# Split weights at drawn offsets in a two-pair ring, operands in unevenly placed groups, in a one-core transformer layer

## The chip, the core and the metric

The kernel runs on one core of a Trainium2 chip. The core has a matrix engine (TensorE, here PE, with its weight loads shown apart as PEld), a vector engine (VectorE, DVE), a scalar engine (ScalarE, ACT), GpSimd (POOL) and a sync engine (SP) that issues the DMAs here. Each works through its own queue in order, and semaphores order the queues against each other. The metric is the device time of one execution in microseconds.

## The reference

One layer of an encoder with 512 tokens and width 2048, all in float32. A conditioning vector gives six modulation vectors. A normalised input is projected to two groups of heads, eight HGRN2 heads (a gated linear recurrence) and eight stick-breaking attention heads. Their outputs go through an output projection and a gated residual. A SwiGLU feed-forward of width 5632 follows.

```python
def reference(x, c, norm1_g, w_in, hg_lb_logits, hg_out_g, sb_q_g, sb_k_g, sb_out_g,
              w_out, norm2_g, w_ffn_in, w_ffn_out, w_ada, b_ada):
...
    for layer in range(DEPTH):
        mod = cond @ w_ada[layer] + b_ada[layer]
        sh1, sc1, g1, sh2, sc2, g2 = [m[:, None, :] for m in jnp.split(mod, N_MOD, axis=-1)]

        h = rms_norm(x, norm1_g[layer]) * (1.0 + sc1) + sh1
        proj = h @ w_in[layer]
        hg_q, hg_f, hg_i, hg_g, sb_q, sb_k, sb_v = jnp.split(proj, IN_SPLITS, axis=-1)
        o_hg = hgrn2_mixer(hg_q, hg_f, hg_i, hg_g, lower_bounds[layer], hg_out_g[layer])
        o_sb = stick_breaking_mixer(sb_q, sb_k, sb_v, sb_q_g[layer], sb_k_g[layer], sb_out_g[layer])
        mixed = jnp.concatenate([o_hg, o_sb], axis=-1).astype(x.dtype) @ w_out[layer]
        x = x + g1 * mixed

        h = rms_norm(x, norm2_g[layer]) * (1.0 + sc2) + sh2
        gate, up = jnp.split(h @ w_ffn_in[layer], 2, axis=-1)
        x = x + g2 * ((jax.nn.silu(gate) * up) @ w_ffn_out[layer])
    return x
```

## The kernel before

Every large product is made from float32 values that are split in two: a high part, which a cast on ACT rounds to the matrix engine's float32r, and a low part, value minus high, which DVE subtracts. Three matmuls stand for one: high weight by high activation, high weight by low activation, low weight by high activation. The method `matmul` of class `Timed` (line 93) issues them all, so all of PE's float32r matmuls have line 93 in the profile, and only the tiles tell them apart.

**Weights.** A raw weight tile of up to 8 KB a partition comes by DMA from SP into one of four buffers (`raw_tile`, line 171, pool `wp`). `split` (line 212) takes one pair of tiles, tags `hi` and `lo`, casts on ACT (line 220) and subtracts on DVE (line 221). The pool has three buffers of each tag (line 137), so three split pairs exist at a time, and a fourth cast must wait until PE has left a slot. A slot is any free one, so a pair may be held. A split holds at most 1024 values a partition. In the feed-forward stages every fourth split goes to a further pair instead: `spare_here` (line 1105, tags `hi2` and `lo2` of pool `tp`) in the first one, `spare_there` (line 1165) in the second, there inside the operand tile `opsB`. The splits stand under a priority raised by `AHEAD` = 300 instructions, and a planner at build time puts the instructions of each engine in an order by priority and by when they are ready in its own model of time. On the chip each queue then keeps that order.

**Stages in order.** (1) v projection of HGRN, 16 steps, 512 columns, accumulators `st`. (2) attention projections, `sb_project` (line 337), 8 heads of 8 splits with 24 matmuls of 384 columns each. (3) HGRN projections, `mtile` (line 599), 8 heads of three products, two splits each with 24 matmuls of 512 columns. The attention and HGRN heads run beside this, set among the matmuls by a clock that the program itself keeps (`Clock`, line 102). (4) output projection, `wo_part` (line 808): for output tiles 0 and 1 all rows but those of the last HGRN head are done first, and their split weights are kept; the upper halves of tiles 2 and 3 follow; when the last head is finished, the kept pairs are used for its row and the loop at line 857 goes on. The activations of stages 1 to 4 lie in two tiles, `hhi` and `hlo` (later `ohi` and `olo`), of 16 rows of 512 values. (5) the gate and up products of the first two blocks of 128 columns (`first_part`, line 959), where the weights of chunk c serve first the first half of the tokens and, after the first product of chunk c + 1, the second half. (6) the first feed-forward stage: for 42 further blocks f, seven products by Strassen's scheme over halves of 8 row tiles (`product`, line 908), each with its own split of 1024 values and 24 matmuls of 256 columns. Their activation operands lie in `opA` (products 1 and 2), `opD` (3), `opB` (6 and 7) and `opC` (5 and 4), high and low alternating by row tile. Results leave PSUM by `tap` (ACT, line 1018), and the forms of the product go out to memory by DMA (line 1095). (7) the second feed-forward stage, `multiply` (line 1183): 12 units, four with three and eight with four tiles of 128 rows, again seven products each, with splits of up to two tiles; a two-tile split is used by 12 matmuls of 512 columns. Here the split weights are the moving operand, and the feed-forward operands, loaded back into `opsA`, `opsB` and `opsC` (`load_op`, line 1028), are the stationary one.

**Where the tiles lie.** This is the compiled program's allocation, in bytes from the start of a partition; the remainder by 512 stands in brackets. Ring, high parts: 43808, 47904, 52000. Ring, low parts: 56096, 60192, 64288 (288 each). `hhi`, `ohi`, `opB`, `opsC`: 68384 (288). `hlo`, `olo`, `opC`, `opsB`: 101152 (288). `opA`, `opsA`: 133920 (288). `opD`: 166688 (288). Spare pair of stage 6: 215008 and 219104 (480). Rows and blocks within them are whole multiples of 512 bytes, so the remainder is the same all through a tile.

Of the kernel before, what the change touches and what calls it, by code (L numbers as in the profile page):

```python
# [10 lines left out]
F32 = mybir.dt.float32  # L11
F32R = mybir.dt.float32r
# [5 lines left out]
P = 128  # L18
D = 2048
KT = 16  # L20
T = 512
# [3 lines left out]
HT = 256  # L25
HALF = 8
# [59 lines left out]
class Timed:  # L86


    def __init__(self, engine, clock):
        self.engine, self.clock = engine, clock  # L90
# [39 lines left out]
def trunk(ctx, tc, a):  # L130
    nc = tc.nc
    V, S, G = nc.vector, nc.scalar, nc.gpsimd
# [74 lines left out]
        nc.sync.dma_start(r, src)  # L207
        return r

    spare, count = [], [0]  # L210

    def split(r, shape, name):
        count[0] += 1
        if spare and count[0] % 4 == 0:
            hi, lo = spare[0](shape, name)
        else:
            hi = wp.tile(shape, F32R, tag="hi", name=name + "h")
            lo = wp.tile(shape, F32R, tag="lo", name=name + "l")
        with tc.high_priority(offset=AHEAD):
            S.copy(hi, r)  # L220
            V.tensor_sub(lo, r, hi.bitcast(F32))  # L221
        return hi, lo
# [30 lines left out]
        newton(y, av, tmp)  # L253


    hhi = hp.tile([P, KT, T], F32R, tag="hhi", name="hhi")
    hlo = hp.tile([P, KT, T], F32R, tag="hlo", name="hlo")
    xo = xop.tile([P, KT, T], F32, tag="xo", name="xo")
    vctx = ctx.enter_context(ExitStack())
    vp = vctx.enter_context(tc.tile_pool(name="vp", bufs=1))  # L260
# [25 lines left out]
    for k in range(KT):  # L286
        xk = xo[:, k]
        if k == 0:
            for i in range(2):
                sl = slice(i * 1024, i * 1024 + 1024)  # L290
                gemv(r0[:, sl], cond[:, sl], lead[:, i:i + 1])
            j = SC1 * KT
            V.scalar_tensor_tensor(mod[:, j:j + 1], lead[:, 0:1], lead[:, 1:2], small_col(C_BADA, j), op0=ALU.add, op1=ALU.add)
            finish_gain(SC1, 0, 1)
            whi = wp.tile([P, 1024], F32R, tag="hi", name="wi0h")
            wlo = wp.tile([P, 1024], F32R, tag="lo", name="wi0l")
# [12 lines left out]
        S.activation(hhi[:, k], xk, AF.Identity, scale=gk)  # L309
        V.scalar_tensor_tensor(hlo[:, k], xk, gk, hhi[:, k].bitcast(F32), op0=ALU.mult, op1=ALU.subtract)  # L310
        if k == 0:
            S.activation(ss1, xk, AF.Square)
        else:
            sq = sb.tile([P, T], F32, tag="qT" if k % 2 else "kT", name=f"sq{k}", bufs=1)
            S.activation(sq, xk, AF.Square)
            V.tensor_add(ss1, ss1, sq)
        for n in range(2):
            for t in range(4):
                ts_ = slice(t * P, t * P + P)
                cs = slice(n * T, n * T + T)  # L320
# [471 lines left out]
        gates[h] = SG  # L792


    ohi = hp.tile([P, KT, T], F32R, tag="hhi", name="ohi")
    olo = hp.tile([P, KT, T], F32R, tag="hlo", name="olo")
    last = NH - 1

    def split_o(k):
# [73 lines left out]

    early = fh.tile([P, 2, HALF, 2, HT], F32R, tag="b1", name="opA")
    H = {1: early[:, 0], 2: early[:, 1], 3: fg.tile([P, HALF, 2, HT], F32R, tag="b22", name="opD")}
    parts = {}

    def block(kh, th, j):  # L880
        return x1[:, kh * HALF + j, th * HT:th * HT + HT]

    def split_to(p, j, src):
        S.copy(H[p][:, j, 0], src)
        V.tensor_sub(H[p][:, j, 1], src, H[p][:, j, 0].bitcast(F32))

    def normed(kh, th, j):
        k, hs = kh * HALF + j, slice(th * HT, th * HT + HT)
# [3 lines left out]
    def make_first(j):  # L892
        for kh in range(2):
            normed(kh, 0, j)
            split_to(1 + kh, j, block(kh, 0, j))
            parts[kh, 0, j] = H[1 + kh][:, j, 0], H[1 + kh][:, j, 1]

    def make_second(j):
        normed(0, 1, j)
        t = ft.tile([P, 2, HT], F32R, tag="t", name=f"b12_{j}")  # L900
        S.copy(t[:, 0], block(0, 1, j))
        V.tensor_sub(t[:, 1], block(0, 1, j), t[:, 0].bitcast(F32))
        parts[0, 1, j] = t[:, 0], t[:, 1]
        normed(1, 1, j)
        split_to(3, j, block(1, 1, j))
        parts[1, 1, j] = H[3][:, j, 0], H[3][:, j, 1]

    def product(out, w, p, first=False):
        whi, wlo = w
        for j in range(HALF):  # L910
            PE.matmul(out, whi[:, j], H[p][:, j, 0], start=first and j == 0, stop=False, skip_group_check=True)
            PE.matmul(out, whi[:, j], H[p][:, j, 1], start=False, stop=False, skip_group_check=True)
            PE.matmul(out, wlo[:, j], H[p][:, j, 0], start=False, stop=j == HALF - 1, skip_group_check=True)

# [66 lines left out]
            with tc.high_priority(offset=AHEAD):  # L981
                hold(0)

    late = hp.tile([P, 2, HALF, 2, HT], F32R, tag="hhi", name="opB")
    later = hp.tile([P, 2, HALF, 2, HT], F32R, tag="hlo", name="opC")
    H.update({6: late[:, 0], 7: late[:, 1], 5: later[:, 0], 4: later[:, 1]})
    for j in range(HALF):
        V.tensor_sub(block(0, 0, j), block(0, 1, j), block(0, 0, j))
        t2 = ft.tile([P, HT], F32, tag="t", name=f"t2_{j}")
# [33 lines left out]

    def place(n):
        n %= 11
        return places[0][:, n] if n < 4 else places[1][:, n - 4] if n < 7 else places[2][:, n - 7]

    def load_op(c, q):
        if c < len(CHUNKS):
# [12 lines left out]
    yraw = []  # L1042

    def begin_second():
        places.append(fh.tile([P, 4, 4, 2, HT], F32R, tag="b1", name="opsA"))
        load_op(0, 0)
        load_y(0, 2)
        load_op(0, 1)
        load_y(0, 0)
        yraw.append(hp.tile([P, 3, 4, T], F32, tag="hhi", name="yraw0"))  # L1050
        load_y(0, 1)
        load_y(0, 3)
        load_op(0, 2)
        load_op(0, 3)
        places.append(hp.tile([P, 4, 4, 2, HT], F32R, tag="hlo", name="opsB"))
        for q in range(4, 7):
            load_op(0, q)
        yraw.append(fg.tile([P, 2, 4, T], F32, tag="b22", name="yraw"))
# [44 lines left out]
            later.pop(0)()  # L1103

    def spare_here(shape, name):
        return [tp.tile(shape, F32R, tag=t, name=name + t, bufs=1) for t in ("hi2", "lo2")]

    spare.append(spare_here)
    count[0] = 0
# [50 lines left out]
    tctx.close()  # L1160


    more = places[1][:, 3].rearrange("p n h t -> p (n h t)")

    def spare_there(shape, name):
        n = shape[1] * shape[2]
# [63 lines left out]
    for u, (c, i) in enumerate(units):  # L1230
# [15 lines left out]
        for q, p in enumerate(ORDER):  # L1246
# [37 lines left out]
            if p == 3:  # L1284
                load_y(u + 1, 3)
            if u == 0 and q == 6:
                places.append(hp.tile([P, 4, 4, 2, HT], F32R, tag="hhi", name="opsC"))
            if q < 4 and i == (c == 0):
                load_op(c + 1, q)
            if i == 1 and 1 <= q < 4:  # L1290
# [61 lines left out]
```

## Time and profile before

| | us |
|---|---|
| runs | 2303.31 and 2305.09 |
| median of the runs | 2304.2 |
| span of the profiled execution | 2299.2 |

The profiled execution's span runs from its first to its last instruction; its own time with what lies around the span is not listed apart, so the span is set against the median of the runs, which is 5.0 us more. The mean granted clock of PE over the span is 0.994 of full speed.

How to read the rows: in the timeline, a row gives the start in microseconds from the beginning of the span, the length, the engine, the line, the operation, the written tile and the read ones, the shapes, and how many like instructions the row merges; in brackets stands how long the engine was idle just before and what released it. Matmuls are pipelined, so their lengths overlap; what counts is from start to start. A name like `ff_5h` is product 5's high weights in the first feed-forward stage; `wfo_2h` those of the second stage for the tiles from 2 on.

### The profile page before, as it was taken

What the parts mean: (1) busy time and instruction counts of PE and PEld (TensorE: products, weight loads), DVE (VectorE), ACT (ScalarE), POOL (GpSimd) and SP (SyncE); (2) the same over time, 40 slices, a digit from 0 to 9 for tenths busy, and PEclk for the clock granted to TensorE, in tenths of its full rate; (3) what the DMA queues carried; (4) which work ended last, traced back from release to release, by engine and by line L of the source; (5) the groups of instructions that cost most, each with busy time, mean ns of one, the idle gap of its engine ahead of it and who ended that gap; (6) DMA issues with size and microseconds to landing.
All of it is one profiled execution on the core that took longest, in us unless ns stands there. A gap on an engine that the chain in (4) does not pass through costs nothing.

```text
span 2299.2 us, 35729 instructions
## 1 busy us (share of the span) xinstructions
PE 2249.4 (98%) x14171; PEld 2050.2 (89%) x14171; DVE 1917.8 (83%) x2566; ACT 1160.6 (50%) x2015; POOL 10.7 (0%) x25
## 2 busy tenths in 40 slices
PE   7999899999999999999999999999999999999999
PEld 6899899888888788999999999999999977778787
DVE  8887779999888865699899988888888778888888
ACT  4316666565655522564454445454545544544453
POOL 0000000000000000000000000000000000000000
PEclk9999999999999999999999999999999999999999
DMA  9885546853322386346555645454443486665452
GB/s 368 319 317 218 174 145 227 304 183 111 128 93 74 130 303 214 105 151 225 189 204 185 220 143 175 143 174 143 150 160 129 166 314 232 238 220 213 154 200 76
DMA packets 114978, 437.69 MB, mean 190 GB/s; under 512 B 9822, under 2 KB 58236, under 8 KB 76796
## 3 DMA queue, kind: packets, MB, share of 16 engines
q1 hardware_dynamic: 114812, 435.42, 53.0%
q8 instruction: 111, 1.82, 0.3%
q14 instruction: 55, 0.45, 0.1%
HBM read 386.61 MB, written 48.77 MB: 189 GB/s over the span
## 4 chain that ended last, share of the span: by engine, by line
PE 77%; DVE 13%; DMA 3%; issue 3%; ACT 3%; SPq 0%; DVEq 0%; ACTq 0%
PE ffA L93 18%; PE foA L93 9%; PE ffC L93 9%; PE sbp L93 7%; PE wo L93 7%; PE foC L93 4%; PE ffB L93 4%; PE st L93 4%; PE hgf L93 4%; PE hgq L93 3%; PE hgg L93 3%; DMA opd<-fhi 1%; DVE ada L180 1%; DVE yraw L1190 1%; PE l L93 1%
## 5 line engine op out<-in xcount | busy, mean ns | idle before, releaser
L180 DVE SCALAR_TENSOR_TENSOR ada<-ada,cond 128x2048 f32<-128x2048 f32 x95 | 216.8, 2286 | 54.5 <-DMA ada<-in_w_ada 54.3
L93 PE MATMUL ffA<-opD,ff_3h 128*128 128x256 f32 x512 | 93.9, 284 | 1.8 <-ACT u L1018 1.7
L93 PE MATMUL ffA<-opB,ff_6h 128*128 128x256 f32 x512 | 94.1, 284 | 1.0 <-ACT ff_6h L220 1.0
L93 PE MATMUL ffB<-opA,ff_2h 128*128 128x256 f32 x512 | 93.5, 283 | 0.0
L93 PE MATMUL ffC<-opC,ff_4h 128*128 128x256 f32 x512 | 93.5, 283 | 0.0
L93 PE MATMUL ffA<-opC,ff_5h 128*128 128x256 f32 x496 | 90.7, 283 | 0.8 <-ACT b L1018 0.8
L93 PE MATMUL ffA<-opA,ff_1h 128*128 128x256 f32 x496 | 90.6, 283 | 0.0
L93 PE MATMUL ffC<-opB,ff_7h 128*128 128x256 f32 x496 | 90.6, 283 | 0.0
L221 DVE TENSOR_TENSOR wfo_0l<-wfo,wfo_0h 128x1024 fp32r<-128x1024 f32 x48 | 58.7, 1224 | 37.9 <-ACT wfo_0h L220 37.5
L93 PEld LDWEIGHTS ffA<-opD,ff_3h 128*128 128x128 f32 x512 | 79.7, 192 | 2.4 <-ACT u L1018 2.4
L93 PEld LDWEIGHTS ffA<-opB,ff_6h 128*128 128x128 f32 x512 | 80.1, 193 | 1.3 <-ACT ff_6h L220 1.2
L93 PEld LDWEIGHTS ffC<-opC,ff_4h 128*128 128x128 f32 x512 | 79.7, 192 | 0.0
L93 PEld LDWEIGHTS ffB<-opA,ff_2h 128*128 128x128 f32 x512 | 79.7, 192 | 0.0
L220 ACT CAST wfo_0h<-wfo 128x1024 fp32r<-128x1024 f32 x48 | 50.6, 1054 | 57.5 <-PE foA L93 50.4
L1092 ACT CAST fhi<-forms 128x512 fp32r<-128x512 f32 (+1 forms) x63 | 43.6, 692 | 68.5 <-DMA opd<-fhi 59.2
L93 PEld LDWEIGHTS ffA<-opC,ff_5h 128*128 128x128 f32 x496 | 77.2, 192 | 1.0 <-ACT b L1018 1.0
L93 PEld LDWEIGHTS ffC<-opB,ff_7h 128*128 128x128 f32 x496 | 77.3, 192 | 0.0
L93 PEld LDWEIGHTS ffA<-opA,ff_1h 128*128 128x128 f32 x496 | 77.2, 192 | 0.0
L93 PE MATMUL ffA<-opB,ff_6l 128*128 128x256 f32 x256 | 72.7, 284 | 0.0
L93 PE MATMUL ffC<-opC,ff_4l 128*128 128x256 f32 x256 | 72.4, 283 | 0.0
L93 PE MATMUL ffA<-opD,ff_3l 128*128 128x256 f32 x256 | 72.4, 283 | 0.0
L93 PE MATMUL ffB<-opA,ff_2l 128*128 128x256 f32 x256 | 72.4, 283 | 0.0
(1646 smaller groups left out, 7764.6 us busy)
## 6 DMA issues: line engine op xcount, KB each, us to landing
ada<-in_w_ada SPq DMA_DIRECT2D x95, 1024.0 KB, 5.2
wfo<-in_w_fo SPq DMA_DIRECT2D x16, 1024.0 KB, 5.9
yraw<-in_w_fo SPq DMA_DIRECT2D x16, 1024.0 KB, 4.8
fix<-in_w_fix SPq DMA_DIRECT2D x14, 1024.0 KB, 5.6
opd<-forms SPq DMA_DIRECT2D x44, 256.0 KB, 4.3
opd<-fhi SPq DMA_DIRECT2D x42, 256.0 KB, 4.3
opsC<-opd SPq DMA_DIRECT2D x10, 1024.0 KB, 5.1
opsA<-opd SPq DMA_DIRECT2D x9, 1024.0 KB, 7.2
```

The source lines that it names most:

```text
L93: self.engine.matmul(out, lhsT, rhs, **kw)
L180: V.scalar_tensor_tensor(w, w, 1.0, row, op0=ALU.mult, op1=ALU.mult, accum_out=col)
L220: S.copy(hi, r)
L221: V.tensor_sub(lo, r, hi.bitcast(F32))
L1092: S.copy(hi, R[:, q])
L1190: V.tensor_sub(*(t[:, k0:k0 + w] for t in (d, e, g)))
```

## The change

The ring in `wp` has two buffers of each tag instead of three (the pool's own number is overridden in `pair_of`). Each is wider, 1144 values instead of 1024, and a split lies in it at an offset drawn at build time from 0 to 15 lines of 8 values (32 bytes); in about half of the draws the low part has the offset of the high part. The spare pair of stage 6 is drawn likewise. The tiles of activations and of feed-forward operands get 128 values more and are cut into two or four groups, each set off by a number of lines of its own, as the tuples in the diff say. High and low operands of products 3 to 7 become separate blocks, where they alternated before. What is computed, and the number of casts, subtractions, matmuls and DMAs, stays as it was.

```diff
-    spare, count = [], [0]
+    spare, count, draw = [], [0], np.random.RandomState(7)
+    LINE = 8
+    SLOT = 1024 + 15 * LINE
+
+    def shifted(t, off, shape):
+        n = int(np.prod(shape[1:]))
+        t = t[:, off:off + n]
...
+        return t
+
+    def pair_of(pool, tags, shape, name, bufs):
+        offs = draw.randint(0, 16, 2)
+        if draw.randint(0, 2):
+            offs[1] = offs[0]
+        return [shifted(pool.tile([P, SLOT], F32R, tag=tag, name=name + tag, bufs=bufs), LINE * int(o), shape)
+                for tag, o in zip(tags, offs)]
+
+    BIG = KT * T + 128
+
+    def grouped(tag, name, n, offs, shape, pool=None, size=BIG):
+        t = (pool or hp).tile([P, size], F32R, tag=tag, name=name)
+        return [shifted(t, i * n + LINE * o, [P] + shape) for i, o in enumerate(offs)]
+
+    class Rows:
...
+            v = self.views[k // 4][:, k % 4]
...
+    def rows_of(tag, name, offs):
+        return Rows(grouped(tag, name, 4 * T, offs, [4, T]))
...
     def split(r, shape, name):
         count[0] += 1
         if spare and count[0] % 4 == 0:
             hi, lo = spare[0](shape, name)
         else:
-            hi = wp.tile(shape, F32R, tag="hi", name=name + "h")
-            lo = wp.tile(shape, F32R, tag="lo", name=name + "l")
+            hi, lo = pair_of(wp, ("hi", "lo"), shape, name, 2)
...
-    hhi = hp.tile([P, KT, T], F32R, tag="hhi", name="hhi")
-    hlo = hp.tile([P, KT, T], F32R, tag="hlo", name="hlo")
+    hhi = rows_of("hhi", "hhi", (0, 1, 3, 6))
+    hlo = rows_of("hlo", "hlo", (0, 1, 3, 8))
...
-    ohi = hp.tile([P, KT, T], F32R, tag="hhi", name="ohi")
-    olo = hp.tile([P, KT, T], F32R, tag="hlo", name="olo")
+    ohi = rows_of("hhi", "ohi", (0, 2, 5, 12))
+    olo = rows_of("hlo", "olo", (0, 2, 5, 10))
...
-    early = fh.tile([P, 2, HALF, 2, HT], F32R, tag="b1", name="opA")
-    H = {1: early[:, 0], 2: early[:, 1], 3: fg.tile([P, HALF, 2, HT], F32R, tag="b22", name="opD")}
+    H = dict(zip((1, 2), grouped("b1", "opA", 4096, (0, 3), [HALF, 2, HT], fh)))
+    H[3] = grouped("b22", "opD", 2048, (5, 7), [HALF, HT], fg, 4096 + 128)
+    for p in (1, 2):
+        H[p] = [H[p][:, :, i] for i in range(2)]
...
-            PE.matmul(out, whi[:, j], H[p][:, j, 0], start=first and j == 0, stop=False, skip_group_check=True)
+            PE.matmul(out, whi[:, j], H[p][0][:, j], start=first and j == 0, stop=False, skip_group_check=True)
...
-    late = hp.tile([P, 2, HALF, 2, HT], F32R, tag="hhi", name="opB")
-    later = hp.tile([P, 2, HALF, 2, HT], F32R, tag="hlo", name="opC")
-    H.update({6: late[:, 0], 7: late[:, 1], 5: later[:, 0], 4: later[:, 1]})
+    late = grouped("hhi", "opB", 2048, (1, 1, 9, 9), [HALF, HT])
+    later = grouped("hlo", "opC", 2048, (2, 2, 4, 12), [HALF, HT])
+    H.update({6: late[0:2], 7: late[2:4], 5: later[0:2], 4: later[2:4]})
...
-        places.append(fh.tile([P, 4, 4, 2, HT], F32R, tag="b1", name="opsA"))
+        places.append(grouped("b1", "opsA", 2048, (0, 3, 6, 10), [4, 2, HT], fh))
...
-        places.append(hp.tile([P, 4, 4, 2, HT], F32R, tag="hlo", name="opsB"))
+        places.append(grouped("hlo", "opsB", 2048, (0, 2, 5, 9), [4, 2, HT]))
...
     def spare_here(shape, name):
-        return [tp.tile(shape, F32R, tag=t, name=name + t, bufs=1) for t in ("hi2", "lo2")]
+        return pair_of(tp, ("hi2", "lo2"), shape, name, 1)
...
-    more = places[1][:, 3].rearrange("p n h t -> p (n h t)")
+    more = places[1][3].rearrange("p n h t -> p (n h t)")
...
-                places.append(hp.tile([P, 4, 4, 2, HT], F32R, tag="hhi", name="opsC"))
+                places.append(grouped("hhi", "opsC", 2048, (0, 1, 4, 12), [4, 2, HT]))
```

More of the change, by code (lines that the diff above doesn't have):

```diff
@@ L208, in load, with __init__, __getitem__ @@
         return r
-    spare, count = [], [0]
+    spare, count, draw = [], [0], np.random.RandomState(7)
[4 more added lines that the diff above has]
+        t = t[:, off:off + n]
+        if len(shape) == 3:
+            t = t.rearrange("p (a b) -> p a b", a=shape[1])
+        elif len(shape) == 4:
+            t = t.rearrange("p (a b c) -> p a b c", a=shape[1], b=shape[2])
+        return t
[10 more added lines that the diff above has]
+    class Rows:
+        def __init__(self, views):
+            self.views = views
+        def __getitem__(self, key):
+            k, r = key[1], key[2:]
+            v = self.views[k // 4][:, k % 4]
+            return v[(slice(None),) + tuple(r)] if r else v
+    def rows_of(tag, name, offs):
+        return Rows(grouped(tag, name, 4 * T, offs, [4, T]))
     def split(r, shape, name):
@@ L294, in trunk @@
             finish_gain(SC1, 0, 1)
-            whi = wp.tile([P, 1024], F32R, tag="hi", name="wi0h")
-            wlo = wp.tile([P, 1024], F32R, tag="lo", name="wi0l")
+            whi, wlo = pair_of(wp, ("hi", "lo"), [P, 1024], "wi0", 2)
             for sl in (slice(0, T), slice(T, 2 * T)):
@@ L883, in split_to @@
     def split_to(p, j, src):
-        S.copy(H[p][:, j, 0], src)
-        V.tensor_sub(H[p][:, j, 1], src, H[p][:, j, 0].bitcast(F32))
+        S.copy(H[p][0][:, j], src)
+        V.tensor_sub(H[p][1][:, j], src, H[p][0][:, j].bitcast(F32))
     def normed(kh, th, j):
@@ L895, in make_first @@
             split_to(1 + kh, j, block(kh, 0, j))
-            parts[kh, 0, j] = H[1 + kh][:, j, 0], H[1 + kh][:, j, 1]
+            parts[kh, 0, j] = H[1 + kh][0][:, j], H[1 + kh][1][:, j]
     def make_second(j):
@@ L905, in make_second @@
         split_to(3, j, block(1, 1, j))
-        parts[1, 1, j] = H[3][:, j, 0], H[3][:, j, 1]
+        parts[1, 1, j] = H[3][0][:, j], H[3][1][:, j]
     def product(out, w, p, first=False):
@@ L910, in product @@
         for j in range(HALF):
-            PE.matmul(out, whi[:, j], H[p][:, j, 0], start=first and j == 0, stop=False, skip_group_check=True)
-            PE.matmul(out, whi[:, j], H[p][:, j, 1], start=False, stop=False, skip_group_check=True)
-            PE.matmul(out, wlo[:, j], H[p][:, j, 0], start=False, stop=j == HALF - 1, skip_group_check=True)
+            PE.matmul(out, whi[:, j], H[p][0][:, j], start=first and j == 0, stop=False, skip_group_check=True)
+            PE.matmul(out, whi[:, j], H[p][1][:, j], start=False, stop=False, skip_group_check=True)
+            PE.matmul(out, wlo[:, j], H[p][0][:, j], start=False, stop=j == HALF - 1, skip_group_check=True)
     m = KT - 1
@@ L1025, in place @@
         n %= 11
-        return places[0][:, n] if n < 4 else places[1][:, n - 4] if n < 7 else places[2][:, n - 7]
+        return places[0][n] if n < 4 else places[1][n - 4] if n < 7 else places[2][n - 7]
     def load_op(c, q):
```

## The prediction

> **What bounds the kernel now.** I read the page first (busy shares, then the chain that ended last), then the table of busy time by stretch, then the timeline of single instructions on PE, ACT and DVE.
>
> ```profile
> span 2299.2 us, 35729 instructions
> PE 2249.4 (98%) x14171; PEld 2050.2 (89%) x14171; DVE 1917.8 (83%) x2566; ACT 1160.6 (50%) x2015; POOL 10.7 (0%) x25
> PE 77%; DVE 13%; DMA 3%; issue 3%; ACT 3%; SPq 0%; DVEq 0%; ACTq 0%
> ...
> 1000.00:1100.00 100.00, 95.13 (x782) 94.32 (x782) 95.83 (x117) 49.40 (x76) 0.00 (x0) 0.98 0.53 185
> 1700.00:1800.00 100.00, 100.00 (x847) 100.00 (x847) 82.54 (x93) 50.62 (x75) 0.00 (x0) 1.00 0.47 158
> 2100.00:2200.00 100.00, 98.41 (x429) 79.72 (x428) 84.79 (x88) 48.90 (x59) 0.00 (x0) 1.00 0.61 221
> ```
>
> PE is busy 98% of the span and carries 77% of the chain. The last three rows are hundred-microsecond stretches of the first and the second feed-forward stage (columns: PE, PEld, DVE, ACT, POOL in percent, granted clock, DMA share, GB/s): PE is saturated at full clock, and DVE, second at 82 to 96%, has little room. So what counts is the interval between two matmuls and every wait of PE. The change touches both.
>
> ```profile
> 1303.62 0.40 PE L93 MATMUL ffA<-opC,ff_5h 128*128 128x256 f32 x2
> 1303.98 0.40 PE L93 MATMUL ffA<-opC,ff_5h 128*128 128x256 f32 x2
> ...
> 1306.50 0.39 PE L93 MATMUL ffC<-opC,ff_4hi 128*128 128x256 f32 x2
> 1306.84 0.39 PE L93 MATMUL ffC<-opC,ff_4hi 128*128 128x256 f32 x2
> ...
> 2048.95 0.62 PE L93 MATMUL foA<-wfo_2h,opsC 128*128 128x512 f32 x2
> 2049.63 0.62 PE L93 MATMUL foA<-wfo_2h,opsC 128*128 128x512 f32 x2
> ...
> 180.09 0.33 PE L93 MATMUL sbp<-wsb_1l,hhi 128*128 128x384 f32 x1
> 185.81 0.33 PE L93 MATMUL sbp<-wsb_2l,hhi 128*128 128x384 f32 x1
> ```
>
> Each row (start, length) is two matmuls of a triple; the third, with the low half, stands between. With weights in the ring (ff_5h) a triple takes 0.36 us, 120 ns a matmul. With weights in the spare pair (ff_4hi; names in hi and lo without a number are the spare) it takes 0.34 us, 113.3 ns. Operand, shape, clock and accumulation are alike; only the home differs. By the allocation shown above, every operand and every ring slot of the kernel starts 288 bytes past a multiple of 512, and the spare pair alone starts 480 past. So equal residues cost 6.7 ns more than residues 192 bytes apart. For 512 columns a triple takes 0.68 us, 226.7 ns a matmul; for 384 columns 33 matmuls lie between the two rows shown, 173.3 ns each. The step from 256 to 512 columns is 106.7 ns, so the part that doesn't depend on width is 13.3 ns at all three widths in the ring and 6.7 ns in the spare.
>
> **The change part by part.**
>
> *Offsets (gain).* They put weights at any of 16 places 32 bytes apart, against operands at uneven places, so the difference modulo 512 is spread over 16 values. Of these the trace shows two: 0 (slow) and 6 places (fast). The slow matmuls, from the loops: feed-forward in 42 x 7 x 24 = 7056 less 73 spare products x 24 = 1752, so 5304; gate and up of the first two blocks 384, last output tile 96, attention 8 x 8 x 24 = 1536, v projection 384, HGRN 24 x 48 = 1152, output projection 15 x 48 = 720, feed-forward out 44 x 42 = 1848. Sum 11424. If all became fast: 11424 x 6.7 ns = 76 us. Bounds: 1 place in 16 slow (gain 71 us) to 15 in 16 slow (gain 5 us, and the spare loses 11). I take a quarter slow, nearer to the first, since a clash of two read streams should need nearby places: 57 us, less 1752 x 6.7 x 1/4 = 3 us on the spare, so 54 us. I take 8 us off where DVE (95.83%, above) leaves PE no room: 46 us.
>
> *Ring of two pairs instead of three (loss).* A split is an ACT cast and a DVE subtraction. Its cast waits until PE has left the slot.
>
> ```profile
> 1318.03 0.40 PE L93 MATMUL ffB<-opA,ff_2h 128*128 128x256 f32 x2
> 1318.39 0.39 PE L93 MATMUL ffA<-opB,ff_6hi 128*128 128x256 f32 x2
> ...
> 1309.51 1.05 ACT L220 CAST ff_2h<-wg17r 128x1024 fp32r<-128x1024 f32 x1
> 1310.56 1.05 ACT L220 CAST ff_6hi<-wg17r 128x1024 fp32r<-128x1024 f32 x1
> 1315.59 1.05 ACT L220 CAST ff_5h<-ffS 128x1024 fp32r<-128x1024 f32 x1
> 1318.53 1.06 ACT L220 CAST ff_4h<-wu17r 128x1024 fp32r<-128x1024 f32 x1 [1.61 <-PE ffB L93]
> ...
> 1302.81 1.22 DVE L221 TENSOR_TENSOR ff_3l<-wg16r,ff_3h 128x1024 fp32r<-128x1024 f32 x1
> 1310.59 1.23 DVE L221 TENSOR_TENSOR ff_2l<-wg17r,ff_2h 128x1024 fp32r<-128x1024 f32 x1
> 1313.47 1.22 DVE L221 TENSOR_TENSOR ff_6lo<-wg17r,ff_6hi 128x1024 fp32r<-128x1024 f32 x1
> 1317.90 1.22 DVE L221 TENSOR_TENSOR ff_5l<-ffS,ff_5h 128x1024 fp32r<-128x1024 f32 x1
> 1320.83 1.21 DVE L221 TENSOR_TENSOR ff_4l<-wu17r,ff_4h 128x1024 fp32r<-128x1024 f32 x1
> ```
>
> The last high matmul of ff_2 starts at 1318.15 (the second of the first row), and the cast into its slot at 1318.53, 0.38 later; in the trace that cast is three products ahead of its use, so nobody waits. With two pairs and a spare at every fourth split, the two splits around the spare keep two products of cover, but the third of each four has one: its slot is left by the product before last. From the last high matmul T: cast T + 0.38 to T + 1.44, subtraction T + 1.47 to T + 2.69. PE goes on at T + 0.24 (1318.39) with one product of 24 matmuls, 2.88 or 2.72 us, and wants the third's low half two matmuls on, at T + 3.36 or T + 3.17. The cover is 0.5 to 0.7 us, and nothing stalls if both engines are free. They are not always: from cast end to subtraction start the rows give 0.03 (ff_2), 1.86 (ff_6), 1.26 (ff_5), 1.24 us (ff_4). Where DVE is late by 1.2 us, PE stands 0.7. With one prompt case in four the mean excess over 0.5 is 0.71 us; the bounds are 0 and that. The split is placed ahead of the other work on DVE (its priority is raised by 300), and now it is the urgent one, so I take 0.3 us: 73 x 0.3 = 22 us. Behind the waiting cast stand on ACT the taps of the PSUM banks, which PE waits for in turn; that is in the upper bound.
>
> In the second feed-forward stage a split of two tiles is used by 12 matmuls (2.72 us), of one tile by 6.
>
> ```profile
> 1894.46 0.39 PE L93 MATMUL foC<-wfo_2h,opsA 128*128 128x512 f32 x1
> 1895.82 0.39 PE L93 MATMUL foA<-wfo_0h,opsA 128*128 128x512 f32 x1
> ```
>
> These rows are a one-tile product, 1.36 us. In the four units of three tiles the third of four follows such a one. A matmul of 512 columns ends 0.39 after its start, so the chain ends at T + 2.80; PE wants the low half at T + 0.23 + 1.36 + 0.23 = T + 1.82. That is 0.98 us each, 56 splits / 4 = 14 times: 14 us. In the eight units of four tiles the cover is 0.4, 28 times, and I take 0.3 again: 8 us. Sum 22 (bounds 14 and 34).
>
> Without a spare, every split has one product of cover. In the v projection, HGRN and output projection that is 24 x 227 ns = 5.4 us against 2.7: nothing. In the attention projection 24 x 173 ns = 4.2 us against less than 2.7: 4 us for late cases (0 to 10). In the first gate and up part a pair of weights serves two products, with another's first product between; two pairs leave the next split no cover if PE keeps its order (6 x 2.4 = 14 us) and one product of 2.88 us if the planner pulls a ready product forward (nearly 0): I take 6.
>
> ```profile
> 797.68 0.47 PE L93 MATMUL wo<-ohi,wo_8h 128*128 128x512 f32 x1
> 804.30 0.50 PE L93 MATMUL wo<-ohi,wo_8h 128*128 128x512 f32 x1 [0.90 <-ACT wo_8h L220]
> 810.70 0.39 PE L93 MATMUL wo<-olo,wo_0h 128*128 128x512 f32 x1
> ```
>
> The output projection holds two pairs (tiles 0 and 1, lower half) until the last HGRN head is finished: the row at 810.70 is the first of their last matmuls. The blocks of tiles 2 and 3 that fill PE until then, from about 798 and 804, go through the third pair. It is gone, so 2 x 24 x 227 ns = 10.9 us of work moves behind that point. Bounds 0 and 13 (with one exposed split); I take 9, because the last head comes a little earlier.
>
> *Operand layout.* As many casts, subtractions, matmuls and DMAs as before, of the same sizes; high and low become separate blocks. Raw weight tiles are freed later by up to a product, so their loads are issued later on SP; four raw tiles cover it, and I cost it at 0 (up to 5 us while the first 100 us run on DMA). PE alone shows the residue: cast and subtraction take 1.05 and 1.22 us for ring and spare alike.
>
> Sum: 22 + 22 + 4 + 6 + 9 = 63 lost, 46 gained, +17 on 2299.2, or 2316. The median of the two runs, 2304.2, stands 5 above the span, so 2321 us, 0.7% slower. That is no change: about 2% either way, under 2258 or over 2350, is what a measurement of this kernel tells from none.
>
> **The rivals.** *The address isn't the cause* (0.13). For it: all fast products share one pair, at the top of the memory, and no ring slot was ever fast. Against it: the 6.7 ns changes exactly at the product's border, for all four operands alike. Then nothing is gained: 2299 + 63 + 5 = 2367, slower. By the Trainium skill, "TensorE: Matmul & The Clock Gate", step-by-step part, weight loads and the moving operand have independent read ports and loading doesn't steal bandwidth from the running matmul; that speaks for this rival, while the trace's two intervals speak against so clean a separation.
>
> *The third split is late* (0.15). Place: the DVE queue when a cast ends. If its subtraction stands behind two others, the 101 thirds (73 + 28) cost 0.9 us instead of 0.3: +61, or 2382, slower. It decides from 0.3 + 29 / 101 = 0.6 us a third. For it: DVE at 82 to 96%, and delays of 1.2 us in three of the four pairs shown. Against it: the raised priority.
>
> *Nearly all places fast, and the third hidden* (0.12). Gain 70.7, lost 9 + 14 = 23: 2304 - 48 = 2256, faster. For it: the cover of 0.5 us. Against it: DVE's load. By the same page of the Trainium skill (part 1) back-to-back matmuls come every N / 2.4 GHz + 2.5 ns, 109 ns for 256 columns: by that estimate the offsets could save 131 us and the time be 2236. No interval in this trace goes under 113.
>
> **How the numbers follow.** My forecast, gain and stalls of the same size, has 0.60, own range 2285 to 2348. Faster 0.12, same 0.60, slower 0.15 + 0.13 = 0.28. The range takes in the rivals on both sides with a tenth left out at either end: 2260 to 2384.
>
> **What would show it.** Right: triples of 0.34 us in many ring products, 0.36 in some, by product; PE waits on L221 and L220 at every third split of four; a gap of about 10 us before the last HGRN head's matmuls in the output projection. Wrong: triples of 0.36 throughout (first rival); PE waits on L221 of over 60 us in the two feed-forward stages (second); almost none (third); or triples under 0.34 or over 0.36, which no row here bounds.

## The result and the profile after

The changed kernel takes 2379.56 us (median of two runs, 2379.47 and 2379.66) beside 2304.2: 1.0325 times as long, 95% interval 1.0295 to 1.0355. That is 75 us slower, where the prediction had 17. The time lies inside the range of the prediction (2260 to 2384), but its forecast was "no change", and the rest of the document is about the 58 us between the two.

The page of the changed kernel, its lines on span, engines and chain:

```profile
span 2377.7 us, 35678 instructions
PE 2293.1 (96%) x14171; PEld 2059.7 (87%) x14171; DVE 1918.9 (81%) x2566; ACT 1163.7 (49%) x2015; POOL 10.1 (0%) x25
PE 50%; DVE 7%; DMA 4%; ACT 2%; issue 2%; DVEq 0%; ACTq 0%
```

The span is 78.5 us longer, yet DVE and ACT work as long as before (1917.8 and 1160.6 us then): no split got slower. PE's busy time grew by 43.7 us with the same number of matmuls, and the rest is idle. How much of that is slower matmuls can't be read from busy time, as the recorded lengths of neighbouring matmuls overlap; the intervals below tell it. The chain's shares sum to 65% only, so it isn't set against the earlier one.

Stretches in the same parts of the two feed-forward stages (columns: PE, PEld, DVE, ACT, POOL in percent, granted clock, DMA share, GB/s):

```profile
1030.00:1130.00 100.00, 96.81 (x795) 95.53 (x794) 94.82 (x114) 49.51 (x76) 0.00 (x0) 0.98 0.53 191
1740.00:1840.00 100.00, 96.84 (x817) 96.44 (x816) 79.36 (x92) 48.79 (x71) 0.00 (x0) 1.00 0.46 156
2200.00:2300.00 100.00, 97.72 (x410) 77.53 (x409) 83.94 (x85) 44.67 (x52) 0.00 (x0) 0.98 0.50 179
```

Late in the first feed-forward stage 817 matmuls fit in 100 us where 847 did; in the second 410 where 429 did. PE's waits by releaser show a part of it (total us, times, longest). These are rows on the preparation of operands, first before, then after:

```profile
PE foC L93 <- DVE wfo_0l L221: 2.4, 2, 1.3
PE ffC L93 <- ACT ff_7hi L220: 2.3, 1, 2.3
```

```profile
PE ffC L93 <- DVE ff_7lo L256: 12.5, 9, 2.7
PE foC L93 <- DVE wfo_0lo L256: 10.5, 13, 1.3
PE sbp L93 <- ACT wsb_6hi L255: 4.5, 1, 4.5
PE foA L93 <- DVE wfo_0lo L256: 3.3, 6, 0.7
PE ff L93 <- ACT b L937: 3.2, 1, 3.2
```

All but the last are waits for split weights, most of all for the low half; the last is one for the high part of an activation (line 937) in the gate and up part, 3.2 us where it had been 0.3. The longest of the first row in the timeline, PE rows first, DVE rows below:

```profile
1312.61 0.39 PE L93 MATMUL ffC<-opB,ff_7lo 128*128 128x256 f32 x1 [2.75 <-DVE ff_7lo L256]
1313.22 0.41 PE L93 MATMUL ffC<-opB,ff_7lo 128*128 128x256 f32 x1
1313.86 0.42 PE L93 MATMUL ffC<-opB,ff_7lo 128*128 128x256 f32 x1
...
1316.37 0.28 PE L93 MATMUL ffC<-opB,ff_7lo 128*128 128x256 f32 x1
1316.72 0.28 PE L93 MATMUL ffC<-opB,ff_7lo 128*128 128x256 f32 x1
...
1310.20 1.23 DVE L1158 TENSOR_TENSOR ffS<-wu16r 128x1024 f32<-128x1024 f32 x1 [2.34 <-DMA wu16r<-in_w_fi]
1311.34 1.22 DVE L256 TENSOR_TENSOR ff_7lo<-wu15r,ff_7hi 128x1024 fp32r<-128x1024 f32 x1
```

Product 7 of block 15 is the (15 - 2) x 7 + 4 = 95th split, the third of its four: the place that the prediction named. DVE stands 2.34 us before an addition for the next block, whose raw weights come late by DMA, and the subtraction that PE wants is queued behind. Then it costs more: after the stop a triple takes 0.64 us (1313.22 to 1313.86), 213 ns a matmul, and 3.7 us after the stop 0.35 us again (1316.37 to 1316.72). The granted clock is 0.50 from 1312.90 to 1316.20 and 1.00 before and after.

The second part is in the matmuls themselves. Two triples of 512 columns after the change:

```profile
2103.90 0.63 PE L93 MATMUL foC<-wfo_0hi,opsC 128*128 128x512 f32 x2
2104.60 0.63 PE L93 MATMUL foC<-wfo_0hi,opsC 128*128 128x512 f32 x2
```

0.70 us, where they took 0.68. To add both parts up, I took the interval from each matmul's start to the next start in the trace. Up to 26 ns over columns / 2.4 ns it counts as matmul time, and its overhead is what it has over columns / 2.4; of a longer one, what goes beyond columns / 2.4 and 13.3 ns counts as a wait, a matmul at half speed included. By stage, from one profiled execution each (a stage runs from its first matmul to that of the next; the last three columns count its own split-product matmuls alone):

| stage | before, us | after, us | waits | matmul time | mean overhead, ns |
|---|---|---|---|---|---|
| v projection, 512 columns | 88.9 | 91.1 | +0.2 | +1.9 | 13.4 to 18.8 |
| attention, 384 | 338.5 | 347.4 | +7.3 | +2.0 | 13.7 to 15.2 |
| HGRN, 512 | 330.5 | 333.3 | -0.7 | +3.5 | 15.0 to 18.5 |
| output projection, 512 | 186.3 | 197.2 | +5.6 | +2.8 | 13.7 to 18.4 |
| first gate and up, 256 | 47.8 | 54.7 | +7.5 | -0.9 | 13.2 to 11.6 |
| first feed-forward, 256 | 845.8 | 864.1 | +20.0 | -2.7 | 11.7 to 11.5 |
| second feed-forward, 512 | 445.7 | 473.8 | +20.2 | +7.0 | 14.2 to 18.8 |

Waits +60 us, matmul time +14 us. The prediction had +63 and -46. The stages differ by 78 us in all; of the 4 us that the two columns leave out, 2.4 stand in stops at the last HGRN head's other matmuls, inside the output projection.

### The profile page after: what moved, and what is told of

It reads as the page before. It is cut to its first block, busy times and chain, and to the rows that moved or that the text cites. A ratio compares the mean times of both kernels' runs of the same rounds, so it can differ in the third digit from the quotient of the medians.

```text
span 2377.7 us, 35678 instructions
## 1 busy us (share of the span) xinstructions
PE 2293.1 (96%) x14171; PEld 2059.7 (87%) x14171; DVE 1918.9 (81%) x2566; ACT 1163.7 (49%) x2015; POOL 10.1 (0%) x25
## 4 chain that ended last, share of the span: by engine, by line
PE 50%; DVE 7%; DMA 4%; ACT 2%; issue 2%; DVEq 0%; ACTq 0%
PE ffA L93 15%; PE foA L93 9%; PE ffC L93 8%; PE wo L93 6%; PE foC L93 5%; PE ffB L93 4%; PE ff L93 2%; DMA opd<-fhi 1%; DVE wfo_0lo L256 1%; PE foB L93 1%; ACT wfo_0hi L255 1%; DMA opd<-forms 1%; DVE wfo L1290 1%; DVE yraw L1226 1%; DVE ff_7lo L256 1%
## 5 line engine op out<-in xcount | busy, mean ns | idle before, releaser
L93 PE MATMUL ffC<-opB,ff_7hi 128*128 128x256 f32 x672 | 124.5, 285 | 0.8 <-ACT ff_7hi L255 0.8
L93 PE MATMUL ffA<-opA,ff_1hi 128*128 128x256 f32 x672 | 122.4, 282 | 1.7 <-ACT ff_1hi L255 1.7
L93 PE MATMUL ffB<-opA,ff_2hi 128*128 128x256 f32 x672 | 121.9, 282 | 1.2 <-ACT ff_2hi L255 1.2
L93 PE MATMUL ffA<-opB,ff_6hi 128*128 128x256 f32 x672 | 121.2, 281 | 0.0
L93 PE MATMUL ffA<-opC,ff_5hi 128*128 128x256 f32 x672 | 121.1, 281 | 0.0
L93 PE MATMUL ffA<-opD,ff_3hi 128*128 128x256 f32 x672 | 121.1, 281 | 0.0
L93 PE MATMUL ffC<-opC,ff_4hi 128*128 128x256 f32 x672 | 120.8, 281 | 0.0
L93 PE MATMUL ffC<-opB,ff_7lo 128*128 128x256 f32 x336 | 96.8, 288 | 12.5 <-DVE ff_7lo L256 12.5
L93 PEld LDWEIGHTS ffC<-opB,ff_7hi 128*128 128x128 f32 x672 | 105.5, 193 | 1.0 <-ACT ff_7hi L255 1.0
L93 PEld LDWEIGHTS ffA<-opA,ff_1hi 128*128 128x128 f32 x672 | 104.1, 190 | 1.9 <-ACT ff_1hi L255 1.9
L93 PEld LDWEIGHTS ffB<-opA,ff_2hi 128*128 128x128 f32 x672 | 103.1, 189 | 1.6 <-ACT ff_2hi L255 1.6
```

The costliest lines, as they stand in the source:

```text
L93: self.engine.matmul(out, lhsT, rhs, **kw)
```

## The experiments

My theory after the result: the third pair costs what the prediction counted, and the uneven homes cost instead of gaining. Rivals: that the ring costs far more and the homes did gain, or that late splits have another cause. Ratios below are against the kernel before on the same chip, with 95% intervals; its median there was 2301.1 to 2302.6 us.

**Ring of two alone.**

```diff
-            hi = wp.tile(shape, F32R, tag="hi", name=name + "h")
-            lo = wp.tile(shape, F32R, tag="lo", name=name + "l")
+            hi = wp.tile(shape, F32R, tag="hi", name=name + "h", bufs=2)
+            lo = wp.tile(shape, F32R, tag="lo", name=name + "l", bufs=2)
...
```

> The kernel before with one edit: the ring of weight halves has two pairs instead of three; every home stays where the rules of before put it (all weights and operands 288 bytes past a multiple of 512). Theory A (the lost third pair costs what the prediction counted, about 60 us of waiting on TensorE, and the uneven homes cost the rest, about 14 us of longer matmul intervals): 2364 us, 2355 to 2373, gaps on TensorE as long as in the changed kernel, a mean interval of a 256-column matmul still about 118.3 ns. Rival B (the ring costs more than counted and the homes gave back the 46 us of the prediction): 2420 us or more. Rival C (the waits come from splits that run slower on uneven homes, the two pairs are nearly enough): 2304 to 2325 us.

2359.33 us, ratio 1.0242 (1.0211 to 1.0274): +58. Theory A. The four runs lie between 2351 and 2366 us, and the profiled one was the fastest, so its trace shows some 50 of the 58. Waits grew by 6.5 us in the attention projection, 7.1 in the first gate and up part, 11.0 in the first and 21.0 in the second feed-forward stage; the output projection took 7.8 us more. The overheads stayed at 11.7 ns for 256 columns in the feed-forward stage and 14.1 for 512. So of the change's ratio of 1.0325 some 0.8% (19 us) is left for the homes; the two ratios have intervals of 0.3% either way.

**Operands alone and draws alone.** In the first the tuples of the change stay (12 lines cut to 10, sizes packed tighter), and the weights go back to a ring of three at one place. In the second the change's weights stay and every tuple becomes zeros.

```diff
# operands alone
-            hi, lo = pair_of(wp, ("hi", "lo"), shape, name, 2)
+            hi = wp.tile(shape, F32R, tag="hi", name=name + "h")
+            lo = wp.tile(shape, F32R, tag="lo", name=name + "l")
...
# draws alone
-    hhi = rows_of("hhi", "hhi", (0, 1, 3, 6))
-    hlo = rows_of("hlo", "hlo", (0, 1, 3, 8))
+    hhi = rows_of("hhi", "hhi", (0, 0, 0, 0))
+    hlo = rows_of("hlo", "hlo", (0, 0, 0, 0))
...
```

> The operand half of the change alone: operands in groups at uneven homes as in the changed kernel (largest shift 10 lines instead of 12, homes packed tighter), a ring of three pairs whose weights all stay at one place, the spare pair as before. Theory A (distances other than 0 modulo 256 bytes cost 2 to 6 ns at 512 columns and give 1 to 2 ns at 256; the ring is whole): 3 to 6 us slower per 1000 matmuls of 512 columns, no new waits: 2301 + 5 to 18, 2306 to 2319 us. Rival B (the drawn offsets of the weights make the slow intervals): 2298 to 2304 us. Rival C (the prediction's gain of 46 us, hidden by the ring in the changed kernel): below 2275 us.

> The weight half of the change alone: the changed kernel with its ring of two pairs, its wide slots and its drawn offsets, all operand shifts set to 0. Theory A (a distance is a distance, whichever side is moved): ring loss of 58 us and 10 to 20 us of longer intervals and late splits, 2369 to 2381 us, as the changed kernel. Rival B (the operands' homes are what costs): 2355 to 2363 us, as the ring of two alone.

2314.02 us, 1.0050 (1.0037 to 1.0064), and 2373.92 us, 1.0314 (1.0292 to 1.0336): theory A both times. Operands alone, with the ring whole, cost 12 us; the draws cost 17 beyond the ring of two (1.0314 beside 1.0242). Both move the mean overhead at 512 columns to 18 or 19 ns, as the change does. Either half scatters the distances, and both together do no more than one.

**What a distance costs.** Two runs read it. The ring of two has slots of 1152 values, which all start at the operands' place modulo 512; the n-th split goes n modulo 16 lines of 32 bytes past it, with both halves or with the low one alone.

```diff
+            t = pool.tile([P, 1152], F32R, tag=tag, name=name + tag, bufs=bufs)[:, 8 * o:8 * o + n]
...
# both halves: offsets s % 16 and s % 16; low half alone: 0 and s % 16
```

> A measuring run: ring of two, all operands at 288 bytes modulo 512 as in the kernel before, the slots of the weight halves 128 bytes wider per side of a multiple of 512, so that the n-th split puts both its hi and its lo half n modulo 16 lines of 32 bytes past that home. It reads the interval of a matmul at each of the 16 distances for 256, 384 and 512 columns, with hi and lo equal. Theory A (rule of the prediction): 13.3 ns of overhead at distance 0, 6.7 ns at the other fifteen. Rival B (a few distances are quick, most are not): 6.7 ns at two to six distances, 13.3 ns or more elsewhere. Rival C (distance isn't it): no order by distance. The total is that of a ring of two, less what the intervals give: 2290 to 2370 us.

> A measuring run as the one with equal halves, but the hi half always stays at the operands' own place modulo 512 and only the lo half moves, n modulo 16 lines of 32 bytes past it. Theory A (each matmul's interval goes by its own two homes): hi matmuls keep 13.3 ns of overhead at all n and only the lo matmul changes, so a mean of about 11 ns. Rival B (the interval goes by how a home stands to that of the matmul beside it, whose weights load meanwhile): a hi matmul that follows or precedes a lo one changes too, and unequal halves cost up to 24 ns, as the smeared intervals of the changed kernel hint. Total 2340 to 2400 us.

The first took 2369.1 us in its one run, the second 2364.93. Mean overhead in ns by distance in lines, both halves alike, with the trace's intervals joined to the program's allocation. The distance is counted from the moving operand's home to the stationary one's. Weights are stationary in HGRN, the output projection and the first feed-forward stage, and moving in the v and attention projections and the second feed-forward stage, where moving them n lines on makes the distance -n.

| columns | 0 | 1 | 2 | 3 | 4 | 5 | 6 | 7 | 8 | 9 | 10 | 11 | 12 | 13 | 14 | 15 |
|---|---|---|---|---|---|---|---|---|---|---|---|---|---|---|---|---|
| 256 | 13.1 | 11.6 | 8.6 | 11.6 | 11.9 | 13.1 | 10.0 | 11.3 | 13.1 | 11.6 | 8.0 | 12.0 | 11.8 | 13.1 | 11.1 | 11.0 |
| 384 | 14.1 | 14.0 | 15.0 | 14.6 | 16.1 | 16.5 | 13.4 | 13.2 | 14.4 | 14.1 | 14.6 | 15.3 | 16.1 | 16.6 | 13.5 | 13.3 |
| 512 | 15.4 | 19.7 | 19.8 | 20.0 | 18.2 | 19.7 | 16.2 | 20.0 | 15.1 | 19.7 | 19.8 | 19.9 | 18.1 | 19.7 | 16.3 | 19.9 |

At 512 columns the row repeats after 8 lines, 256 bytes, and 0 is the best place there is. At 256 columns distances 2 and 10 gain, the others little; the 10.0 at 6 is mostly the spare pair, and the ring's own products there have 11.1. The rule of the prediction and a rule of no order both fall; rival B of the first run (a few quick places) holds in kind for 256 columns, with 8 ns instead of its 6.7, and for no other width. In this run each split stands one line past the one before it, so that a value may hold something of its neighbour's; the row for 256 columns is to be read with that in mind. The average over the 16 places is 11.4 ns for 256 columns, against the 11.7 that the kernel before had with a quarter of its products in the spare, and 18.6 for 512, against 14.1: 4.5 ns on 4104 matmuls of 512 columns are 18 us lost and nothing gained. The border shows in the timeline of the run with both halves moved, where a split at the operands' own place (wfo_0) is followed by one a line further on (wfo_2):

```profile
2035.28 0.62 PE L93 MATMUL foA<-wfo_0hi,opsB 128*128 128x512 f32 x2
2035.96 0.62 PE L93 MATMUL foA<-wfo_0hi,opsB 128*128 128x512 f32 x2
...
2037.34 0.63 PE L93 MATMUL foA<-wfo_2hi,opsB 128*128 128x512 f32 x2
2038.04 0.63 PE L93 MATMUL foA<-wfo_2hi,opsB 128*128 128x512 f32 x2
```

0.68 and 0.70 us for a triple, with shapes, operand and clock alike. With the low half alone moved, matmuls of 512 columns whose own distance is 0 went from 14 to a mean of 17 ns in the second feed-forward stage: the neighbour's home counts too (rival B of that run). By the Trainium skill, "TensorE: Matmul & The Clock Gate", step-by-step part, loading the next weights takes no read bandwidth from the running matmul; these intervals, 0.68 beside 0.70 us, don't agree with homes that are free of each other. Which part of the chip the two share is not shown.

**All at six lines.** If 6 lines made the spare pair quick, 6 lines everywhere should do it. Padding ahead of the operands and in the spare pair puts every matmul there, with a ring of three.

```diff
+    padp = ctx.enter_context(tc.tile_pool(name="padp", bufs=1))
+    padp.tile([P, 80], F32, name="pad")
     hp = ctx.enter_context(tc.tile_pool(name="hp", bufs=1))
...
```

> The kernel before, with its ring of three, and 320 bytes of padding ahead of the operands and inside the spare pair: every FP32r matmul then has its stationary and its moving tile 192 bytes (6 lines of 32) apart modulo 512, as the spare pair had in the kernel before; all homes of one kind stay equal. Theory A (the rule of the prediction, a matmul is quick when the two homes differ modulo 512: overhead 6.7 ns instead of 13.3): all 11,400 FP32r matmuls gain up to 6.7 ns, at most 76 us, so 2228 to 2260 us, 256-column matmuls at 113.3 ns and 512-column ones at 220 ns. Rival B (distance alone isn't what made the spare pair quick): 2295 to 2315 us with intervals as before. Rival C (a distance that is quick for 256 columns is slow for 384 and 512, as the changed kernel's 18 ns overhead at 512 columns hints): 256-column matmuls gain 5304 times 6.7 ns, 36 us, and 4100 512-column ones lose 5 ns each, 21 us: about 2290 us.

2312.58 us, 1.0043 (1.0029 to 1.0056): slower, so theory A falls. Rival B has the total, if not the intervals: 512 columns got slower, as rival C had it, by 1.4 to 6.6 ns of mean overhead from stage to stage. The table tells which: where weights are stationary the distance is 6 (16.2), and HGRN has 16.2 and the output projection 15.7; where they move it is -6, which is 10 (19.8), and the v projection and the second feed-forward stage have 20.0. Here the operands were moved and for the table the weights, so it is the distance that counts and not the place of either. But at 256 columns, too, the gain is small, 11.7 to 10.8 ns, although the spare pair of before had 6.7 at the same distance. Product by product the trace shows why: of 287 whole products 24 ran at 113.4 ns and 263 at 117.8, nothing between. From a product to the next without a stop of PE the rhythm was kept 273 times of 273; over a stop it changed 6 times of 13. In the kernel before, each spare product followed one at distance 0 and ran at 113.4 in 69 of 72 cases. So the same distance has two steady rhythms, and what ran before decides.

**A product at distance 0 as the key.** Then ring products at 6 lines and spare products at 0, in the first feed-forward stage alone, should run quick.

```diff
-    late = hp.tile([P, 2, HALF, 2, HT], F32R, tag="hhi", name="opB")
+    late = by_two(wide_home("hhi", "opB", 80, KT * T + 80))
...
-        return [tp.tile(shape, F32R, tag=t, name=name + t, bufs=1) for t in ("hi2", "lo2")]
+        n = shape[1] * shape[2]
+        return [tp.tile([P, 1152], F32R, tag=t, name=name + t, bufs=1)[:, 32:32 + n].rearrange("p (k d) -> p k d", k=shape[1])
+                for t in ("hi2", "lo2")]
...
```

> The kernel before with its ring of three; only homes differ, all of one kind equal: in the first feed-forward stage (and the gate and up part ahead of it) the operands start 192 bytes (6 lines) below the ring's home modulo 512, the spare pair starts at the operands' own place, and every other stage keeps distance 0. Theory A (a run of 256-column matmuls keeps a rhythm from product to product; at a distance of 6 lines both 113.3 and 117.8 ns are such rhythms, and a product at distance 0 ahead of it leads into the fast one, as in 69 of the 72 spare products of before): ring products at 113.3 ns, spare ones at 120, mean 115.0 instead of 118.3, (5304 - 1752) x 6.7 ns = 24 us of matmul time less, of which some 7 are lost again to waits in the first 200 us of the stage, as in the padded kernel: 2284 us beside 2301 (2278 to 2290). Rival B (the rhythm isn't set by what ran before): ring products at 117.8, mean 118.3, 2298 to 2306 us. Rival C (VectorE is the bound in that stage): intervals as in A, but PE's waits grow by as much, 2298 to 2306 us.

2296.1 us, 0.9973 (0.9964 to 0.9983). The rhythm does what theory A says: after a product at 0 and without a stop, 63 of 64 ring products are quick, in all 188 of 215; the mean is 115.4 ns instead of 118.4. The same two ways of placing weights in the timeline, first with all at 6 lines, then here:

```profile
1401.20 0.40 PE L93 MATMUL ffA<-opA,ff_1h 128*128 128x256 f32 x2
1401.55 0.40 PE L93 MATMUL ffA<-opA,ff_1h 128*128 128x256 f32 x2
```

```profile
1400.38 0.39 PE L93 MATMUL ffC<-opB,ff_7h 128*128 128x256 f32 x2
1400.72 0.39 PE L93 MATMUL ffC<-opB,ff_7h 128*128 128x256 f32 x2
...
1407.54 0.40 PE L93 MATMUL ffA<-opD,ff_3hi 128*128 128x256 f32 x2
1407.90 0.40 PE L93 MATMUL ffA<-opD,ff_3hi 128*128 128x256 f32 x2
```

0.35 us a triple (three times 117.8 ns); 0.34 with ff_7h at 6 lines; 0.36 with the spare ff_3hi, now at 0. But the total isn't A's 2284. The stage lost 21.2 us of matmul time and got back 15.9 as waits, as rival C had it in kind. PE's waits from 1080 to 1860 us:

```profile
PE ffA L93 <- ACT u L1027: 4.2, 4, 1.9
PE ffC L93 <- ACT c L1027: 3.7, 8, 0.8
PE ffA L93 <- ACT b L1027: 2.6, 6, 0.7
```

They are for copies out of PSUM on ACT, not for split weights.

**Every third split.** To test the third of four as the cause of the waits, one constant of the changed kernel was changed.

```diff
-        if spare and count[0] % 4 == 0:
+        if spare and count[0] % 3 == 0:
```

> The changed kernel with one constant changed: every third split of the two feed-forward stages goes to the spare pair instead of every fourth, so that with two pairs in the ring each slot is again left two products before it is filled. Homes stay drawn. Theory A (the waits are those of the third split of four, whose slot is left only by the product before last): PE's waits on the low halves in the two stages fall from 31 us to under 8, and of the 40 us of gaps that these stages gained 25 to 40 go: 2340 to 2355 us. Rival B (the splits are late because VectorE is busy, wherever their slot is): 2370 to 2382 us.

2319.43 us, 1.0079 (1.0062 to 1.0096): 57 us less than the change by the two ratios, more than theory A's 25 to 40. Rival B is out. PE's longest totals of waits from 1040 us on:

```profile
PE foA L93 <- ACT O L1241: 2.4, 1, 2.4
PE foB L98 <- DVE O L1258: 1.0, 1, 1.0
PE ffA L93 <- ACT a L1054: 0.9, 1, 0.9
PE ffC L93 <- DVE ff_7lo L256: 0.7, 1, 0.7
```

The 12.5 us for ff_7lo are 0.7. DVE still stands for late raw weights (11.8 us in that stage, 14.5 in the changed kernel), and PE no longer feels it. What was not expected: the waits fell below those of the kernel before, 3.5 against 10.3 us in the first stage and 5.9 against 17.4 in the second, and this with two pairs and a spare instead of three and a spare.

**The same rotation with equal homes, with three pairs, and with the key.** The first is the ring of two with every third split in the spare. The second, whose edit is shown, keeps three pairs until the feed-forward stages and there uses two of them and the spare in turn. The third adds the homes of the run with the key.

```diff
-        if spare and count[0] % 4 == 0:
+        if spare and count[0] % 3 == 0:
             hi, lo = spare[0](shape, name)
+        elif not spare and count[0] % 3 == 2:
+            hi = wp.tile(shape, F32R, tag="hi3", name=name + "h", bufs=1)
+            lo = wp.tile(shape, F32R, tag="lo3", name=name + "l", bufs=1)
         else:
-            hi = wp.tile(shape, F32R, tag="hi", name=name + "h")
-            lo = wp.tile(shape, F32R, tag="lo", name=name + "l")
+            hi = wp.tile(shape, F32R, tag="hi", name=name + "h", bufs=2)
+            lo = wp.tile(shape, F32R, tag="lo", name=name + "l", bufs=2)
...
```

> The kernel before, all homes equal, with two pairs in the ring and every third split of the feed-forward stages in the spare pair. Beside the changed kernel with the same rotation (2319) it shows what the homes cost once the late third split is gone. Theory A (uneven homes cost some 15 to 20 us wherever they are, mostly 384- and 512-column matmuls): 2319 - 19 = 2300 us, 2295 to 2305, feed-forward gaps of about 10 us in all. Rival B (uneven homes cost nothing without waits): 2315 to 2322 us.

> The kernel before with all its homes; three pairs until the feed-forward stages, and there two of them and the spare in turn (every third split in the spare) in place of three and the spare. Theory A (with three slots in turn the casts that wait for a slot no longer stand ahead of the copies out of PSUM on ScalarE, as the run with every third split showed: gaps of the two stages 9 us instead of 28; and a third instead of a quarter of the first stage's products runs at 113.3 ns, 4 us): 2302 - 19 - 4 = 2279 us, 2273 to 2287. Rival B (the short gaps of that run came from its slower matmuls, which leave the other engines time): 2296 to 2306 us.

> The same rotation with the homes of the lock run: ring products of the first feed-forward stage at a distance of 6 lines, spare products at 0. Theory A (two products of three at 113.3 ns; with the waits for copies out of PSUM gone, most of the saving reaches the end): 4704 instead of 1752 quick matmuls are 20 us less matmul time than in the kernel before, with the 19 us of gaps 2263 us, and up to 10 us of it lost where VectorE has no room: 2263 to 2278 us. Rival B (as in the lock run, two thirds of what matmuls save comes back as waits): 2276 to 2284 us, no better than the same rotation with equal homes.

2305.33 us, 1.0015 (1.0002 to 1.0028): beside 1.0079 with the change's homes, uneven homes cost 0.6%, some 15 us, with hardly a late split in the feed-forward stages of either kernel. That is 0.3 us above theory A's range and far below rival B's 2315. Then 2285.63 us, 0.9931 (0.9917 to 0.9944), again theory A, though waits fell by 10 us in the two stages and not by 19. Then 2277.07 us, 0.9901 (0.9883 to 0.9919), the best version found, 1.0% faster than the kernel before. The time lies within theory A's 2263 to 2278 and also within rival B's 2276 to 2284, so the total doesn't tell them apart; the waits do. The longest from 1080 to 1860 us in the first feed-forward stage:

```profile
PE ffA L93 <- ACT a L1030: 1.8, 2, 1.3
PE ffA L93 <- DVE ff_6l L224: 0.6, 2, 0.3
PE ffC L93 <- DVE ff_4l L224: 0.3, 1, 0.3
```

Of 18.9 us less matmul time in the first stage 4.3 came back as waits, not 15.9 of 21.2 and not rival B's two thirds: with three slots in turn ACT's copies are hardly late any more. That the casts of a fourth slot stand ahead of those copies in ACT's queue is argued from these waits; no run isolated it.

## Why the prediction was wrong

- **The gain of the offsets: the step that failed.** The prediction took 13.3 ns as the price of equal remainders and 6.7 as that of unequal ones, knew two of sixteen distances, and took a quarter of the places as slow, on the ground that a clash of two read streams should need nearby places, which no row bore out: -46 us after a deduction for DVE. Measured: +14 us of matmul time in the change, +12 in all (operands alone), +15 (same rotation, uneven against equal homes), +17 (draws against ring of two), +19 (change against ring of two). Two inferences were false. The spare's 113.3 ns wasn't the price of its distance: at that distance 117.8 is as steady, and the spare was quick because a product at distance 0 ran ahead of it (the runs at six lines and with the key). And the quick case was seen at 256 columns only; at 512 columns distance 0 is the best, and 4104 of the 11424 matmuls that were to gain are of that width. The deduction for DVE's load rested on that gain and had nothing to act on here.
- **The ring: right, and nearly in size.** 63 us were counted, 58 measured for the ring alone, 60 of waits in the change. By term: attention 4 counted, 6.5 measured; first gate and up 6 and 7.1; output projection 9 and 7.8; second feed-forward 22 and 21.0; first feed-forward 22 and 11.0 alone, but 20.0 in the change. Two of these came near by another path than the counted one, which is luck. In attention it is mostly one stop of 4.3 us, for the cast of wsb_6. In the gate and up part it is not late splits of each chunk but one stop of 3.2 us for an activation (line 901) with some 20 matmuls at half speed behind it: before, the product of chunk 2 ran there, and with two pairs it has no weights yet.
- **The third split of four: right.** Waits stood where it says and went with one constant. What was not priced: raw weights that come later (costed at 0, up to 5). DVE stood 14.5 us for them in that stage, against 4.9 before, and in the row shown that is what made a split late by 2.75 us. Nor was the slower matmul after a stop: at half speed ran some 56 matmuls of the two feed-forward stages, in runs of two and more, against 21 before, which cost 7.3 against 2.6 us.
- **The rivals.** "The address isn't the cause" gave 2367 and is the nearest in kind, nothing gained and the ring paid; its reason is wrong, as the address does count. "The third split is late" gave 2382 and was nearest to 2379.56, for a reason that didn't hold: it had 124 us of losses less the 46 of gain, and the waits were 60.
- **What would show it.** "Triples of 0.34 us in many ring products" was named as the sign that it is right: 4 of 285 whole products of the first stage ran under 115 ns after the change, against 69 of 287 before, and 231 between 115 and 119. "Over 0.36, which no row here bounds" was named as the sign that it is wrong; it came at the other width, 0.70 for 0.68 us.

## What to carry to other kernels

An interval that is quick in one place of a kernel is evidence for that place, its width and what runs before it; before it is multiplied by eleven thousand, a run that sets all of them to the quick value is worth more than any reasoning about ports. Count a ring by how many uses lie between leaving a slot and filling it, at each place of the rotation: in the feed-forward stages the uneven turn cost, not the missing pair, and three slots in even turn beat four. Where PE gets quicker, look at the copies out of PSUM next.

## What the runs showed of the hardware

- FP32r matmuls with new weights each time have an overhead that goes by the distance of the two operands' homes, from the moving to the stationary one, repeating after 256 bytes at 384 and 512 columns: at 512 columns 15 ns at 0 and 20 at most other places, at 256 columns 8 to 13.
- A chain of such matmuls keeps a rhythm over many products: at 6 lines 113.4 or 117.8 ns, unchanged over 273 of 273 borders without a stop. A product at distance 0 led into the quick one 63 times of 64, and a stop changed it 6 times of 13.
- After PE had stood for 2.75 us, matmuls of 256 columns went at 213 ns, half speed, for some 3.5 us, with a granted clock of 0.50. The length of the stop alone doesn't decide: in the same trace stops of 2.29 us (to 1480.43) and of 1.25 us (to 2090.87, after one of 0.26) were followed by a granted clock of 0.50, and one of 2.44 us (to 1808.61) by 1.00. The Trainium skill, "TensorE: Matmul & The Clock Gate", part 1, has the clock halved after an idle window of about 3.4 us and freed after as long a busy one: the second agrees with the rows, while the first was reached here with shorter stops.
